# Mamba-2 branch of a hybrid decoder trunk: gates of two groups projected into token rows, with values, outputs and normed outputs turned through VectorE squares and HBM, and dt turned two weights later

## The chip, the cores and the metric

The kernel runs on one core of a Trainium2 chip. The metric is the device time of one execution in microseconds (us), as the median of several runs. A profile is taken of one further execution; its span runs from the first to the last instruction on the core.

Names used below: TensorE (PE in the profile, PEld for its weight loads), VectorE (DVE), ScalarE (ACT), GpSimd (POOL), SyncE (SP).

## The reference

One layer: two parallel token mixers (HGRN2 and Mamba-2), cross-attention into 256 memory tokens, a gated feed-forward block, norms between. All is float32, 256 tokens, model width 2048. The Mamba-2 branch, which is what changes, has 8 groups of 4 heads of 64 values:

```python
xbc = silu(causal_dwconv(xbc_raw, conv_w, conv_b))
xs, bm, cm = split(xbc)                     # 2048 values, 8 x 128, 8 x 128
dt = softplus(dt_raw + dt_bias)             # 32 heads
y = ssd_chunk_scan(xs * dt, dt * A, bm, cm)
y = y + d_skip * xs
y = y * silu(z)
y = y * rsqrt(mean(y * y, over the group's 256 values) + 1e-5)
y = y * norm_g
```

## The kernel before, in words

**Projections.** Each matrix of weights is read once from HBM in pieces of 1 MB (128 rows by 2048 columns), in the order of the list `order` (L87 to L110). `issue` (SyncE) loads a piece two ahead of its use; ScalarE rounds it to a high part (`hi`, L133) and VectorE takes the rest (`lo`, L134), each in two halves of 1024 columns. A pool of five halves holds them, so casts for a piece wait until TensorE has let an earlier half go. TensorE multiplies hi by the hi and lo parts of the activations, and lo by the hi parts.

There are two ways to use a piece. `project` (L241) keeps a 128x128 block of weights in the array and streams tokens: 16 matmuls of 512 columns (the 256 tokens' hi and lo parts side by side) and 16 of 256 columns; the result has channels in rows and tokens in columns, in two halves that `join` (L264) adds: a ScalarE copy `jt` and a VectorE add. `project_tok` (L249) keeps activations in the array and streams 512 columns of weights: over four pieces 96 matmuls of 512 columns, with tokens in rows and no join.

**Order of the work.** Every call of `weights` (one per piece) first runs `step`, which advances the generators in `background` by one stage, and then issues the casts of a later piece. Matmuls that a stage emits are held in their order among themselves; the projections' matmuls, which are not held, are placed around them when the program is built, as are the instructions of the other engines. The result is a fixed order on each engine.

**Mamba-2 before.** `m2_dt` (L661) projects dt for the 32 heads, computes softplus and the running sum, sends the sum to HBM (L680), and has TensorE turn dt and the sum into token rows (L683, L684), with two VectorE copies (L686, L687). `m2_project` (L692) projects six pieces per group: two of values x, one each of B and C, which go through the convolution (L702, L705), and two of gates z. `m2_scan` (L713), a background generator, runs in four stages one or two pieces apart: (A) one Silu over all six (L714) and the decays (L719 to L724); (B) B times C on TensorE (L729, L730), the mask products (L733, L737), a TensorE turn of x into token rows (L742), and x times dt (L745); (C) the 16 matmuls of decays and values (TensorE tile `yp`), d_skip (L759), the product with the gate (L761), squares (L763); (D) a TensorE matmul with ones, which sums the squares over channels (L769), the inverse root (L285, L286), and the norm weights (L773) and the split for the next projection (L281, L282).

**HGRN2**, which the change leaves as it is, already turns its outputs in another way: `turned` (L498) transposes 32x32 squares on VectorE (L503), writes them to HBM by four GpSimd transfers (L506), reads the result back (L509), and `split_turned` (L512) takes it up. Its last head runs beside `m2_dt`.

Of the kernel before, what the change touches and what calls it, by code (L numbers as in the profile page):

```python
# [19 lines left out]
P = 128  # L20
T = 256
# [43 lines left out]
def hybrid_trunk(ctx, tc, xT, memT, par, cst, msk, w_k0, w_ka, w_va, w_hg, w_hv, w_hog, w_ghg, w_bhg, w_dt,  # L65
                 w_m2, w_gm2, w_bm2, w_out, w_q, w_o, w_up, w_dn, fin_g, outT):
# [431 lines left out]
    def turned(y):  # L498

        yq = mp.tile([P, T], F32, name="yq", bufs=1)
        V.transpose(out=yq, in_=y)  # L503
# [4 lines left out]
        yc = mp.tile([P, T], F32, name="yc", bufs=2)  # L508
        G.dma_start(out=yc, in_=yd)  # L509
        return yc  # L510
# [8 lines left out]
    def hg_scan(h, kq, zz, v, sg):  # L519
# [119 lines left out]
        yc = turned(y)  # L639
# [18 lines left out]
    dt_tok = cp.tile([P, 2, 32], F32, name="dt_tok")  # L658
    cum_tok = cp.tile([P, 2, 32], F32, name="cum_tok")

    def m2_dt():  # L661
        ps = project(s2)
        raw = mp.tile([P, T], F32, name="t", bufs=1)
# [5 lines left out]
        V.scalar_tensor_tensor(out=raw[0:32], in0=raw[0:32], scalar=0.0, in1=w[0:32],  # L669
                               op0=ALU.max, op1=ALU.add)  # L670
# [6 lines left out]
        cum = mp.tile([P, T], F32, name="y", bufs=1)  # L677
        V.tensor_tensor_scan(out=cum[0:32], data0=one[0:32], data1=w[0:32], initial=0.0,
                             op0=ALU.mult, op1=ALU.add)
        nc.sync.dma_start(out=cum_d, in_=cum[0:32])  # L680
        ps = pm_.tile([P, 512], F32, name="misc")
        for g in range(2):
            PE.transpose(ps[:, 32 * g:32 * g + 32], raw[0:32, g * P:(g + 1) * P], eye[0:32, 0:32])  # L683
            PE.transpose(ps[:, 64 + 32 * g:96 + 32 * g], cum[0:32, g * P:(g + 1) * P],  # L684
                         eye[0:32, 0:32])
        V.tensor_copy(out=dt_tok, in_=ps[:, 0:64].rearrange("p (g h) -> p g h", g=2))  # L686
        V.tensor_copy(out=cum_tok, in_=ps[:, 64:128].rearrange("p (g h) -> p g h", g=2))  # L687
# [3 lines left out]

    def m2_project(g):  # L692
        sz = mp.tile([P, 6, T], F32, name="sz", bufs=2)
        cb = mp.tile([P, 4, T], F32, name="vc", bufs=2)
        nc.sync.dma_start(out=cb, in_=cum_d[4 * g:4 * g + 4, :].partition_broadcast(P))
        for i in range(4):
            c = m2_chunk(g, i)
            ps = project(s2)
            raw = mp.tile([P, T], F32, name="t", bufs=1)
            join(mp, ps, raw)  # L700
            o = sz[:, i, :]
            S.activation(out=o, in_=raw, func=AF.Identity, bias=pc("m2_cb", c),  # L702
                         scale=pc("m2_cw", 4 * c + 3))
            for s in range(1, 4):
                V.scalar_tensor_tensor(out=o[:, s:T], in0=raw[:, 0:T - s],  # L705
                                       scalar=pc("m2_cw", 4 * c + 3 - s), in1=o[:, s:T],
                                       op0=ALU.mult, op1=ALU.add)
        for i in range(4, 6):
            ps = project(s2)
            join(mp, ps, sz[:, i, :])  # L710
        return sz, cb

    def m2_scan(g, sz, cb):  # L713
        S.activation(out=sz, in_=sz, func=AF.Silu)  # L714
# [10 lines left out]
        yield True  # L725
        yield True
# [12 lines left out]
        tp = pl.tile([P, 512], F32, name="lev")  # L739
        for q in range(2):  # L740
            for i in range(2):
                PE.transpose(tp[:, q * T + i * P:q * T + (i + 1) * P],  # L742
                             sz[:, i, q * P:(q + 1) * P], eye)
        xd = mp.tile([P, 2, T], F32, name="bb", bufs=1)
        V.tensor_tensor(out=xd.rearrange("p q (h c) -> p q h c", c=64),  # L745
                        in0=tp.rearrange("p (q h c) -> p q h c", q=2, c=64),
                        in1=free(dt_tok, 4 * g, [(32, 2), (1, 4), (0, 64)]), op=ALU.mult)
# [9 lines left out]
        y = mp.tile([P, 2, T], F32, name="kq", bufs=2)  # L757
        for i in range(2):
            V.scalar_tensor_tensor(out=y[:, i, :], in0=sz[:, i, :], scalar=pc("m2_d", 2 * g + i),  # L759
                                   in1=yp[:, i * T:(i + 1) * T], op0=ALU.mult, op1=ALU.add)  # L760
        V.tensor_tensor(out=y, in0=y, in1=sz[:, 4:6, :], op=ALU.mult)  # L761
        sq = mp.tile([P, 2, T], F32, name="bb", bufs=1)
        S.activation(out=sq, in_=y, func=AF.Square)  # L763
        V.tensor_tensor(out=sq[:, 0, :], in0=sq[:, 0, :], in1=sq[:, 1, :], op=ALU.add)
        yield True
        if g + 1 < GROUPS:
            yield True
        ps = pm_.tile([P, 512], F32, name="misc")
# [17 lines left out]
    scan = m2_scan(0, *m2_project(0))  # L786
# [14 lines left out]
    for g in range(1, GROUPS):  # L801
        background.append(m2_scan(g, *m2_project(g)))
# [356 lines left out]
def _layout(inp):  # L1159
# [4 lines left out]
    z = _cols(cut(8192, 2048)).reshape(GROUPS, 2, P, 2048)  # L1164
# [20 lines left out]
    def put(name, a):  # L1185
# [35 lines left out]
        "w_m2": np.concatenate([xs, b, c, z], 1), "w_gm2": _toks(cut(16416, 2048)),  # L1221
# [24 lines left out]
```

## Time and profile before

| what | value |
|---|---|
| median of 3 runs | 2253.9 us (2253.28 to 2255.61) |
| the profiled execution: its time, its span | 2255.94 us, 2254.2 us |
| PE busy over the span | 2239.0 us, 99% |
| PEld busy | 1927.9 us, 86% |
| DVE busy | 1623.8 us, 72% |
| ACT busy | 1379.2 us, 61% |
| POOL busy | 45.3 us, 2% |
| mean granted TensorE clock | 0.997 |

Times in the profile are counted from the start of the span. The Mamba-2 branch lies between about 532 us (dt) and 992 us, with the HGRN2 branch's output projections between 578 and 713 us. A row of the timeline gives start, length, engine, line, operation, tile written and tiles read, shapes, and how many were merged; in brackets stands the idle time before it and who ended it. A row of the groups gives line, engine, operation, tiles, shapes, count, busy us, mean ns, and the idle time before with its releasers. The windows give busy us of each engine in a stretch, the granted clock of TensorE, and the DMA share.

### The profile page before, as it was taken

The page shows a single profiled execution, that of the slowest core. Times are in us where ns is not written, and L with a number is a line of the kernel's source. Part 1 is how long each engine was busy: PE and PEld are TensorE (multiplying, and loading weights), DVE is VectorE, ACT ScalarE, POOL GpSimd, SP SyncE. Part 2 cuts the span into 40 slices and gives each one's busy share as a digit, 9 for nine tenths or more (in the row PEclk, how much of TensorE's full clock was granted, in tenths as well). Part 3 has the DMA queues.
Part 4 walks back from the last instruction along what each step waited for, and adds up shares of the span by engine and source line. Part 5 has one row for each costly group of instructions (what it writes and reads, how often), then busy time and mean ns, then how long its engine had stood idle before and what let it go on. Part 6 is the DMA issues. An engine that isn't in the chain of part 4 may idle for free.

```text
span 2254.2 us, 33570 instructions
## 1 busy us (share of the span) xinstructions
PE 2239.0 (99%) x13188; PEld 1927.9 (86%) x13188; DVE 1623.8 (72%) x2602; ACT 1379.2 (61%) x2123; POOL 45.3 (2%) x89
## 2 busy tenths in 40 slices
PE   9999999999999999999999999999999999999998
PEld 8888888887888888888888888888888888888887
DVE  8868878887546677754567765677777777779787
ACT  7567677788546778764456654556555555555554
POOL 0000101100000000000000000000000000000000
PEclk9999999999999999999999999999999999999999
DMA  8645555555655555455566544576555555555554
GB/s 307 245 175 187 183 194 179 182 178 178 219 188 185 189 179 193 180 176 198 187 222 222 210 168 168 178 223 211 193 192 193 193 187 187 188 202 208 207 213 159
DMA packets 89502, 441.11 MB, mean 196 GB/s; under 512 B 25824, under 2 KB 30464, under 8 KB 40320
## 3 DMA queue, kind: packets, MB, share of 16 engines
q1 hardware_dynamic: 69600, 432.36, 53.7%
q0 software_dynamic: 2816, 4.20, 0.7%
q10 hardware_dynamic: 16928, 2.42, 0.6%
q8 instruction: 103, 1.69, 0.3%
q14 instruction: 55, 0.45, 0.1%
HBM read 430.52 MB, written 10.52 MB: 196 GB/s over the span
## 4 chain that ended last, share of the span: by engine, by line
PE 96%; ACT 2%; DVE 1%; issue 0%; DMA 0%; SPq 0%; DVEq 0%
PE proj L82 87%; PE misc L82 5%; PE lev L82 4%; ACT hi L133 0%; DVE lo L134 0%; DMA raw<-in_w_k 0%; DVE e L551 0%; PE lev L811 0%; PE lev L742 0%; ACT L286 0%; ACT L285 0%; ACT h L791 0%; ACT y L638 0%; DVE e L564 0%; PE lev L891 0%
## 5 line engine op out<-in xcount | busy, mean ns | idle before, releaser
L134 DVE TENSOR_TENSOR lo<-raw,hi 128x1024 fp32r<-128x1024 f32 x738 | 894.3, 1223 | 453.2 <-ACT hi L133 403.7
L133 ACT CAST hi<-raw 128x1024 fp32r<-128x1024 f32 x737 | 769.7, 1048 | 425.4 <-PE proj L82 396.6
L82 PE MATMUL proj<-s,hi 128*128 128x512 f32 x3696 | 874.4, 391 | 1.3 <-ACT hi L364 1.1
L82 PEld LDWEIGHTS proj<-s,hi 128*128 128x128 f32 x3696 | 684.9, 188 | 139.2 <-ACT hi L364 2.0
L82 PE MATMUL proj<-hi,s 128*128 128x512 f32 x1962 | 615.2, 390 | 0.0
L82 PEld LDWEIGHTS proj<-s,lo 128*128 128x128 f32 x3696 | 463.6, 191 | 12.1 <-ACT s L281 0.5
L82 PE MATMUL proj<-s,lo 128*128 128x256 f32 x3696 | 471.4, 283 | 0.0
L82 PEld LDWEIGHTS proj<-hi,s 128*128 128x128 f32 x1962 | 368.1, 188 | 76.5 <-issue 0.3
L82 PE MATMUL proj<-lo,s 128*128 128x512 f32 x981 | 382.0, 389 | 0.4 <-DVE lo L134 0.4
L82 PEld LDWEIGHTS proj<-lo,s 128*128 128x128 f32 x981 | 184.2, 188 | 38.2 <-DVE lo L134 0.8
L266 ACT COPY jt<-proj 128x256 f32<-128x256 f32 x183 | 67.7, 370 | 101.4 <-PE proj L82 100.8
L168 ACT CAST hi<-raw 128x1024 fp32r<-128x1024 f32 (+1 forms) x56 | 52.1, 944 | 56.9 <-DVE raw L177 29.9
L169 DVE TENSOR_TENSOR lo<-raw,hi 128x1024 fp32r<-128x1024 f32 (+1 forms) x56 | 60.4, 1088 | 6.6 <-ACT hi L168 5.9
L705 DVE SCALAR_TENSOR_TENSOR sz<-t,par_t,sz 128x255 f32<-128x255 f32 (+2 forms) x96 | 46.2, 481 | 7.4 <-ACT sz L702 5.9
L978 DVE SCALAR_TENSOR_TENSOR gc<-g,par_t,gc 128x255 f32<-128x255 f32 x88 | 42.3, 481 | 2.0 <-ACT gc L976 0.6
L506 POOL DMA_DIRECT2D y_d<-yq x64 | 34.9, 552 | 393.6 <-DVE sm L610 300.2
L82 PE MATMUL proj<-hi,ha 128*128 128x512 f32 x104 | 36.7, 389 | 0.0
L981 ACT ACTIVATE gc<-gc 128x256 f32<-128x256 f32 x44 | 18.4, 417 | 29.9 <-DVE gc L978 29.9
L551 DVE TENSOR_TENSOR e<-bb 128x256 f32<-128x256 f32 x96 | 35.0, 419 | 0.1
L564 DVE TENSOR_TENSOR e<-e,kq 128x256 f32<-128x256 f32 x96 | 34.9, 418 | 0.0
L982 DVE TENSOR_TENSOR gc<-gc,r_f 128x256 f32<-128x256 f32 x44 | 18.7, 425 | 20.9 <-ACT gc L981 20.9
L555 ACT ACTIVATE e<-e 128x768 f32<-128x768 f32 x32 | 27.1, 845 | 10.5 <-DVE e L551 10.0
(302 smaller groups left out, 1765.7 us busy)
## 6 DMA issues: line engine op xcount, KB each, us to landing
raw<-in_w_up SPq DMA_DIRECT2D x88, 1024.0 KB, 4.8
raw<-in_w_m SPq DMA_DIRECT2D x48, 1024.0 KB, 4.8
raw<-in_w_dn SPq DMA_DIRECT2D x44, 1024.0 KB, 4.8
raw<-in_w_hg SPq DMA_DIRECT2D x32, 1024.0 KB, 4.8
raw<-in_w_hv SPq DMA_DIRECT2D x16, 1024.0 KB, 5.0
raw<-in_w_hog SPq DMA_DIRECT2D x16, 1024.0 KB, 4.8
raw<-in_w_ghg SPq DMA_DIRECT2D x16, 1024.0 KB, 4.8
raw<-in_w_bhg SPq DMA_DIRECT2D x16, 1024.0 KB, 4.8
```

The lines of the kernel that those rows point to most:

```text
L82: ins = PE.matmul(*args, **kwargs)
L133: S.copy(out=hi[:, c - a:d - a], in_=raw[:, c:d])
L134: V.tensor_tensor(out=lo[:, c - a:d - a], in0=raw[:, c:d], in1=hi[:, c - a:d - a].bitcast(F32), op=ALU.subtract)
L168: S.copy(out=hi[:, 0:d - c], in_=raw[:, c:d])
L169: V.tensor_tensor(out=lo[:, 0:d - c], in0=raw[:, c:d], in1=hi[:, 0:d - c].bitcast(F32), op=ALU.subtract)
L266: S.copy(out=tmp, in_=ps[:, T:2 * T])
L506: G.dma_start(out=yd.rearrange("(n i) (b f) -> b i n f", i=B, b=P // B)[b], in_=yq[b * B:(b + 1) * B, :].rearrange("i (n f) -> i n f", n=P ...
L551: V.tensor_tensor(out=lev[hw].rearrange("p (n c i) -> p n c i", c=2, i=hw), in0=free(bb, 0, [(2 * hw, nb), (T + hw, 2), (1, hw)]), in1=fre ...
L555: S.activation(out=e[j], in_=e[j], func=AF.Exp)
L564: V.tensor_tensor(out=ev, in0=ev, in1=free(kq, 0, [(2 * hw, nb), (T + hw, 2), (1, hw)]), op=ALU.mult)
L705: V.scalar_tensor_tensor(out=o[:, s:T], in0=raw[:, 0:T - s], scalar=pc("m2_cw", 4 * c + 3 - s), in1=o[:, s:T], op0=ALU.mult, op1=ALU.add)
L978: V.scalar_tensor_tensor(out=gc[:, s:T], in0=g[:, 0:T - s], scalar=pc("f_cw", 3 * c + 2 - s), in1=gc[:, s:T], op0=ALU.mult, op1=ALU.add)
```

## The change

Gates z are no longer projected in `m2_project`. A new `m2_gates` projects the gates of two groups at once with `project_tok` (four pieces), ahead of the even group's values, and the columns are put into an order in which the later squares fit. Silu of the gates is applied in the even group's stage A. Stage A now also turns x: Silu writes x in a mixed order, `turned` transposes its squares, and a GpSimd transfer brings it back in token rows. Stage B takes x times dt from there, with no TensorE turn. Stage C turns the outputs into token rows in the same way, so that the gate, the squares (with a sum along the row) and the inverse root are worked out there with one number for each token, with no matmul with ones. Stage D turns the normed outputs back, and a stage E takes them up with `split_turned`. In `m2_dt`, the turn of dt and its sum into token rows moves to a generator of its own, two pieces later, with its matmuls held in order; `dt_tok` holds each number twice.

```diff
-    order += [w_dt[0]] + [w_m2[0, i] for i in range(6)]
+    order += [w_dt[0]] + [w_z[0, i] for i in range(4)] + [w_m2[0, i] for i in range(4)]
...
-        order += [w_m2[g, i] for i in range(6)]
+        order += [w_z[g // 2, i] for i in range(4) if g % 2 == 0] + [w_m2[g, i] for i in range(4)]
...
-    def turned(y):
+    def turned(y, n, name):
-        yq = mp.tile([P, T], F32, name="yq", bufs=1)
+        yq = mp.tile([P, 64 * n], F32, name="yq", bufs=1)
         V.transpose(out=yq, in_=y)
-        yd = dp.tile([P, T], F32, name="y_d", bufs=4)
+        yd = dp.tile([n * B, T], F32, name=name, bufs=4)
         for b in range(P // B):
             G.dma_start(out=yd.rearrange("(n i) (b f) -> b i n f", i=B, b=P // B)[b],
-                        in_=yq[b * B:(b + 1) * B, :].rearrange("i (n f) -> i n f", n=P // B))
+                        in_=yq[b * B:(b + 1) * B, :].rearrange("i (n f) -> i n f", n=n))
+        return yd
...
         nc.sync.dma_start(out=cum_d, in_=cum[0:32])
+        background.append(m2_dt_rows(raw, cum))
+
+    def m2_dt_rows(raw, cum):
+        yield from pause(2)
         ps = pm_.tile([P, 512], F32, name="misc")
...
+    def m2_gates():
+        zt = mp.tile([P, 2, 512], F32, name="sg", bufs=2)
+        for q, ps in enumerate(project_tok(s2)):
+            S.copy(out=zt[:, q, :], in_=ps)
+        return zt
...
-        for i in range(4, 6):
-            ps = project(s2)
-            join(mp, ps, sz[:, i, :])
...
-    def m2_scan(g, sz, cb):
-        S.activation(out=sz, in_=sz, func=AF.Silu)
+    def m2_scan(g, sz, cb, zt):
+        yield from pause(0 if g in (0, GROUPS - 1) else 1 + 2 * (g % 2))
+        xc = mp.tile([P, 2 * T], F32, name="w", bufs=1)
+        xv = xc.rearrange("p (m i t) -> p i m t", i=2, t=B)
+        S.activation(out=xv, in_=sz[:, 0:2, :].rearrange("p i (m t) -> p i m t", t=B), func=AF.Silu)
+        S.activation(out=sz[:, 2:4, :], in_=sz[:, 2:4, :], func=AF.Silu)
+        if g % 2 == 0:
+            S.activation(out=zt, in_=zt, func=AF.Silu)
+        yd = turned(xc, T // B, "x_d")
+        x = mp.tile([P, 2, T], F32, name="kq", bufs=2)
+        G.dma_start(out=x, in_=yd.rearrange("(q p) c -> p q c", p=P))
...
-        tp = pl.tile([P, 512], F32, name="lev")
...
-                PE.transpose(tp[:, q * T + i * P:q * T + (i + 1) * P],
-                             sz[:, i, q * P:(q + 1) * P], eye)
...
-        V.tensor_tensor(out=y, in0=y, in1=sz[:, 4:6, :], op=ALU.mult)
-        sq = mp.tile([P, 2, T], F32, name="bb", bufs=1)
-        S.activation(out=sq, in_=y, func=AF.Square)
-        V.tensor_tensor(out=sq[:, 0, :], in0=sq[:, 0, :], in1=sq[:, 1, :], op=ALU.add)
...
-        mm(ps[:, 0:T], lhsT=ones, rhs=sq[:, 0, :], start=True, stop=True)
-        r = mp.tile([P, T], F32, name="r", bufs=1)
-        rsqrt(r, ps[:, 0:T], 1.0 / T, eps2_t)
+        yd = turned(y, T // B, "x_d")
+        yt = mp.tile([P, 2, T], F32, name="bb", bufs=1)
+        G.dma_start(out=yt, in_=yd.rearrange("(q p) c -> p q c", p=P))
+        yield from pause(2)
...
+            V.tensor_tensor(
...
+            S.activation(out=yt[:, q, :].rearrange("p (n c) -> p n c", c=B), in_=yv[:, q],
+                         func=AF.Square, accum_out=r[:, q:q + 1])
+        rsqrt(r[:, 2:4], r[:, 0:2], 1.0 / T, eps2_t)
+        for q in range(2):
+            S.activation(out=yv[:, q], in_=yv[:, q], func=AF.Copy, scale=r[:, 2 + q:3 + q])
+        yd = turned(y, T // B, "x_d")
+        yc = mp.tile([P, 2, T], F32, name="yc", bufs=2)
+        G.dma_start(out=yc, in_=yd.rearrange("(i p) t -> p i t", p=P))
+        yield from pause(2)
         for i in range(2):
-            V.scalar_tensor_tensor(out=y[:, i, :], in0=y[:, i, :], scalar=pc("m2_g", 2 * g + i),
-                                   in1=r, op0=ALU.mult, op1=ALU.mult)
-            split(ym[:, 2 * g + i, :], y[:, i, :])
+            split_turned(ym[:, 2 * g + i, :], yc[:, i, :], pc("m2_g", 2 * g + i))
```

**How the order moves.** On TensorE, at dt's projection (`s_76` holds the normed input, `cst_t` the unit matrix, `misc<-vc,a` is an HGRN2 head's last product; the rows with - are of before, with + of after):

```order
 L82 MATMUL proj<-s_76,hi 128x512 x16
-L82 MATMUL proj<-s_76,lo 128x256 x32
-L82 MATMUL proj<-s_76,hi 128x512 x25
-L683 MATMUL misc<-cst_t,t 128x32
-L82 MATMUL proj<-s_76,hi 128x512 x7
-L82 MATMUL proj<-s_76,lo 128x256 x2
-L684 MATMUL misc<-cst_t,y 128x32
-L683 MATMUL misc<-cst_t,t 128x32
-L684 MATMUL misc<-cst_t,y 128x32
+L82 MATMUL proj<-s_76,lo 128x256 x16
 L82 MATMUL misc<-vc,a_1178 128x128 x3
```

The four turns of dt (`t`) and its sum (`y`) leave the middle of the following projection; after, they stand as L687 behind head 15's product, with that head's scores and two pieces of the gates' projection between dt's own matmuls and them.

On VectorE at the same place, before (`t` is dt, `y` the running sum, `lf` a helper):

```order
L665 TENSOR_SCALAR t<-t,par_t 32x256
L134 TENSOR_TENSOR lo<-raw,hi 128x1024
L669 SCALAR_TENSOR_TENSOR t<-t,lf 32x256
L134 TENSOR_TENSOR lo<-raw,hi 128x1024
L673 TENSOR_SCALAR lf<-t,an 32x256
L678 SCALAR_TENSOR_TENSOR y<-r,lf 32x256
L267 TENSOR_TENSOR t<-proj,jt 128x256
L686 COPY dt_tok<-misc 128x64
L687 COPY cum_tok<-misc 128x64
```

and after (`bb` holds dt and its sum, `a` the head's scores):

```order
L618 COPY a_1179<-sm 32x2x32 x4
L669 SCALAR_TENSOR_TENSOR bb<-bb,lf 32x256
L673 TENSOR_SCALAR lf<-bb,an 32x256
L677 SCALAR_TENSOR_TENSOR bb<-r,lf 32x256
L134 TENSOR_TENSOR lo<-raw,hi 128x1024
L502 STREAM_TRANSPOSE yq<-y 128x256
L134 TENSOR_TENSOR lo<-raw,hi 128x1024 x2
L628 TENSOR_TENSOR y<-misc,sg 128x2x4x32
L691 COPY dt_tok<-misc 128x128
L692 COPY cum_tok<-misc 128x64
```

Two `lo` casts stood inside dt's chain, and the next join of a projection behind it had to wait for the turns, which read the same tile `t`. Now no cast stands inside the chain; the first one behind it is the second half of the gates' third piece, and the tile that the turns read is no longer `t`.

On ScalarE in stage A of a group, before (group 4, counting from 0; `e` are the decays, `vc` and `cum_tok` the running sums):

```order
L719 ACTIVATE e_9186<-vc,cum_tok 128x256
L721 ACTIVATE e_9186<-vc,cum_tok 128x128
L719 ACTIVATE e_9186<-vc,cum_tok 128x256
L721 ACTIVATE e_9186<-vc,cum_tok 128x128
L719 ACTIVATE e_9187<-vc,cum_tok 128x256
L133 CAST hi<-raw 128x1024
L721 ACTIVATE e_9187<-vc,cum_tok 128x128
L719 ACTIVATE e_9187<-vc,cum_tok 128x256
L133 CAST hi<-raw 128x1024
L763 ACTIVATE bb<-kq 128x512
L721 ACTIVATE e_9187<-vc,cum_tok 128x128
L724 ACT_TABLE_LOAD
```

and after (group 6: the last twelve rows of the stretch between two casts):

```order
L739 ACTIVATE e_9685<-vc,cum_tok 128x256
L741 ACTIVATE e_9685<-vc,cum_tok 128x128
L739 ACTIVATE e_9685<-vc,cum_tok 128x256
L741 ACTIVATE e_9685<-vc,cum_tok 128x128
L744 ACT_TABLE_LOAD
L744 ACTIVATE e_9684<-e_9684 128x768
L715 ACTIVATE sz<-t,par_t 128x256
L729 ACT_TABLE_LOAD
L729 ACTIVATE sz<-sz 128x512
L744 ACT_TABLE_LOAD
L744 ACTIVATE e_9685<-e_9685 128x768
L133 CAST hi<-raw 128x1024
```

Casts stood among the decays before. In this stretch of after none does: seven rows stand ahead of the twelve shown (four more decays, a table load, a Silu and a convolution start), and four table loads are among the 18 instructions between two casts. Over the whole program the ScalarE order holds 64 table loads, where before's holds 56.

More of the change, by code (lines that the diff above doesn't have):

```diff
@@ L638, in hg_scan @@
             S.activation(out=yv[:, g], in_=yv[:, g], func=AF.Copy, scale=r[:, 2 + g:3 + g])
-        yc = turned(y)
+        yd = turned(y, P // B, "y_d")
+        yc = mp.tile([P, T], F32, name="yc", bufs=2)
+        G.dma_start(out=yc, in_=yd)
         yield from pause(gap)
@@ L662, in m2_dt @@
         ps = project(s2)
-        raw = mp.tile([P, T], F32, name="t", bufs=1)
+        rows = mp.tile([P, 2, T], F32, name="bb", bufs=1)
+        raw, cum = rows[:, 0, :], rows[:, 1, :]
         join(mp, ps, raw)
@@ L680, in m2_dt @@
         nc.sync.dma_start(out=cum_d, in_=cum[0:32])
+        background.append(m2_dt_rows(raw, cum))
+    def m2_dt_rows(raw, cum):
+        yield from pause(2)
         ps = pm_.tile([P, 512], F32, name="misc")
         for g in range(2):
[L683 to L686, printed above, removed]
+            for o, x in ((0, raw), (64, cum)):
+                ins = PE.transpose(ps[:, o + 32 * g:o + 32 * g + 32], x[0:32, g * P:(g + 1) * P],
+                                   eye[0:32, 0:32])
+                tc.keep_in_program_order(ins)
+        V.tensor_copy(out=dt_tok, in_=free(ps, 0, [(32, 2), (1, 32), (0, 2)]))
         V.tensor_copy(out=cum_tok, in_=ps[:, 64:128].rearrange("p (g h) -> p g h", g=2))
@@ L738, in m2_scan @@
                             op=ALU.mult)
-        tp = pl.tile([P, 512], F32, name="lev")
+        xd = mp.tile([P, 2, T], F32, name="bb", bufs=1)
         for q in range(2):
-            for i in range(2):
-                PE.transpose(tp[:, q * T + i * P:q * T + (i + 1) * P],
-                             sz[:, i, q * P:(q + 1) * P], eye)
[L744 to L747, printed above, removed]
+            V.tensor_tensor(out=xd[:, q, :].rearrange("p (i b c) -> p i b c", i=2, c=B),
+                            in0=x[:, q, :].rearrange("p (b i c) -> p i b c", i=2, c=B),
+                            in1=free(dt_tok, 64 * q + 8 * g, [(4, 2), (1, 4), (0, B)]), op=ALU.mult)
         yield True
@@ L762, in m2_scan @@
[L762 to L771 removed]
+            V.scalar_tensor_tensor(out=yv[:, i], in0=xv[:, i], scalar=pc("m2_d", 2 * g + i),
+                                   in1=yp[:, i * T:(i + 1) * T].rearrange("p (m t) -> p m t", t=B),
+                                   op0=ALU.mult, op1=ALU.add)
@@ L772, in m2_scan @@
+        rsqrt(r[:, 2:4], r[:, 0:2], 1.0 / T, eps2_t)
+        for q in range(2):
+            S.activation(out=yv[:, q], in_=yv[:, q], func=AF.Copy, scale=r[:, 2 + q:3 + q])
+        yd = turned(y, T // B, "x_d")
+        yc = mp.tile([P, 2, T], F32, name="yc", bufs=2)
+        G.dma_start(out=yc, in_=yd.rearrange("(i p) t -> p i t", p=P))
+        yield from pause(2)
         for i in range(2):
-            V.scalar_tensor_tensor(out=y[:, i, :], in0=y[:, i, :], scalar=pc("m2_g", 2 * g + i),
-                                   in1=r, op0=ALU.mult, op1=ALU.mult)
@@ L801, in hybrid_trunk @@
     for g in range(1, GROUPS):
[L802 removed]
+        if g % 2 == 0:
+            zt = m2_gates()
+        background.append(m2_scan(g, *m2_project(g), zt))
     def turn(c):
```

31 lines of the change are left out of this document (16 added, 15 removed).

## Prediction

> **What bounds the kernel now.** I read the page's first part, then who waited for whom on TensorE, then the windows of the Mamba-2 stage.
>
> ```profile
> PE 2239.0 (99%) x13188; PEld 1927.9 (86%) x13188; DVE 1623.8 (72%) x2602; ACT 1379.2 (61%) x2123; POOL 45.3 (2%) x89
> ```
> ```profile
> PE misc L683 <- DVE t L669: 3.1, 1, 3.1
> ```
> ```profile
> 756.41:939.57 183.16, 183.16 (x1092) 160.06 (x1091) 137.57 (x211) 145.37 (x215) 0.00 (x0) 1.00 0.51 183
> ```
>
> TensorE is busy 99% of the span, and its longest wait on another engine is one of 3.1 us, at the turn of dt (L683). The window is five Mamba-2 groups of 36.63 us each: TensorE never idles, VectorE is busy 137.57/5 = 27.5 us of a group, ScalarE 145.37/5 = 29.1. So what the change takes off TensorE comes off the span, as long as the two casting engines keep up; ScalarE, with 36.6 - 29.1 = 7.5 us free per group, is the tighter one.
>
> **TensorE, group by group.** A group on TensorE, in starts, lengths and counts:
>
> ```profile
> 757.06 0.60 PE L742 MATMUL lev<-cst_t,sz 128*128 128x128 f32 x4
> 757.42 2.15 PE L82 MATMUL proj<-s,lo 128*128 128x256 f32 x16
> ...
> 772.25 3.82 PE L82 MATMUL proj<-s,hi 128*128 128x512 f32 x16
> 775.91 0.59 PE L82 MATMUL misc<-bb,ones 128*128 128x256 f32 x2
> 776.15 4.03 PE L82 MATMUL proj<-s,hi 128*128 128x512 f32 x16
> 780.01 4.00 PE L82 MATMUL proj<-s,lo 128*128 128x256 f32 x32
> 783.85 7.44 PE L82 MATMUL proj<-s,hi 128*128 128x512 f32 x32
> 791.13 2.08 PE L82 MATMUL proj<-s,lo 128*128 128x256 f32 x16
> ```
>
> Durations of matmuls overlap, so I take distances between starts. 32 lo matmuls take 783.85 - 780.01 = 3.84 us, 32 hi matmuls 791.13 - 783.85 = 7.28 us: a piece in channel rows costs (3.84 + 7.28)/2 = 5.56 us.
>
> A piece in token rows, from a stretch of HGRN2's output projection where each 0.68 us holds three matmuls of 512 columns:
>
> ```profile
> 591.88 0.39 PE L82 MATMUL proj<-lo,s 128*128 128x512 f32 x1
> ...
> 597.32 0.39 PE L82 MATMUL proj<-lo,s 128*128 128x512 f32 x1
> ```
>
> Eight triples lie between the two rows, the 24 matmuls of one piece: 597.32 - 591.88 = 5.44 us.
>
> - Gates: 16 pieces go from channel rows to token rows, 16 x (5.56 - 5.44) = **1.9 us** saved.
> - The four turns of x (L742): 757.42 - 757.06 = 0.36 us per group, eight times: **2.9 us** saved.
> - The matmul with ones: from 772.25 to 780.01 are 7.76 us with 32 hi matmuls, which alone take 7.28; 0.48 us per group, eight times: **3.8 us** saved.
>
> The other matmuls of a group stay. That is 8.6 us; a group costs TensorE 36.63 - 8.6/8 = 35.56 us after.
>
> **dt.** These rows are from the place where dt is turned, and two from a head's block without trouble.
>
> ```profile
> 509.12 0.83 PE L82 MATMUL misc<-vc,a 128*128 128x128 f32 x6
> ...
> 511.36 0.50 PE L82 MATMUL proj<-hi,s 128*128 128x512 f32 x1
> ```
> ```profile
> 532.17 4.00 PE L82 MATMUL proj<-s,lo 128*128 128x256 f32 x32
> 536.01 5.86 PE L82 MATMUL proj<-s,hi 128*128 128x512 f32 x25
> 544.92 0.31 PE L683 MATMUL misc<-cst_t,t 32*128 32x32 f32 x1 [3.06 <-DVE t L669]
> 545.16 3.35 PE L82 MATMUL proj<-s,hi 128*128 128x512 f32 x7
> ...
> 552.43 3.86 PE L82 MATMUL proj<-s,lo 128*128 128x256 f32 x30
> 556.13 2.68 PE L82 MATMUL proj<-s,hi 128*128 128x512 f32 x11
> 559.47 0.91 PE L82 MATMUL misc<-vc,a 128*128 128x128 f32 x6 [0.66 <-DVE a L621]
> ```
> ```profile
> 547.16 0.68 DVE L678 TENSOR_TENSOR_SCAN y<-r,lf 32x256 f32<-32x256 f32 x1
> ```
> ```profile
> 545.00:546.00 1.00, 1.00 (x3) 0.84 (x4) 0.35 (x1) 1.00 (x2) 0.00 (x0) 0.50 0.55 164
> ```
>
> From 532.17 to 552.43 are 20.26 us. In them stand 32 lo (3.84), 32 hi (25 ahead of L683, 7 behind it: 7.28), 2 lo (0.24), the four small turns (at most 0.45), and head 14's product with head 15's scores, which take 511.36 - 509.12 = 2.24 elsewhere: 14.05 us. So 6.2 us are lost: 3.06 of waiting, and the rest because the granted clock (the first 0.50 of the window's row) is half behind the wait: 7 hi take 3.35 us there where full speed makes 1.6. At 559.47 a head's product comes 0.84 us late (11 hi from 556.13 end at 556.13 + 2.50 = 558.63). Together **7.0 us**.
>
> The Trainium skill ("TensorE: Matmul & The Clock Gate", Part 1) has the clock fall to half after an idle window of about 3.4 us; here 3.06 us were enough, and by a strict 3.4 us there would be no slow stretch to win back.
>
> After, the turns stand behind two pieces and the head's block. dt's own matmuls before ended with the first 16 lo, at 532.17 + 1.92 = 534.1; the running sum was there at 547.84, 13.7 us later, with two casts inside its chain that are gone. The turns are due 2.24 + 2 x 5.44 = 13.1 us behind dt's end, and head 15's product (0.83 in the row at 509.12) stands ahead of them too: 13.9 us. So the chain is just covered, at its length of before; I leave 0.5 us for it. The write of the running sum (L680) keeps its place on SyncE's queue at the end of the chain, and the weight loads queued behind it wait no longer than before; its readers (`vc`) stand four pieces later than they did.
>
> Sum of what can go: 1.9 + 2.9 + 3.8 + 7.0 = **15.6 us**.
>
> **What it costs: ScalarE.** Rows of one group (756.41 to 793.04) by mean ns and idle before, then three of HGRN2's last heads:
>
> ```profile
> L266 ACT COPY jt<-proj 128x256 f32<-128x256 f32 x6 | 2.2, 364 | 2.4 <-PE proj L82 2.4
> L714 ACT ACTIVATE sz<-sz 128x1536 f32<-128x1536 f32 x1 | 1.5, 1490 | 0.6 <-DVE sz L267 0.6
> L285 ACT ACT_TABLE_LOAD x1 | 1.3, 1283 | 0.0
> L763 ACT ACTIVATE bb<-kq 128x512 f32<-128x512 f32 x1 | 0.6, 627 | 0.0
> L719 ACT ACTIVATE e<-vc,cum_tok 128x256 f32<-128x256 f32 x4 | 2.0, 496 | 0.0
> L721 ACT ACTIVATE e<-vc,cum_tok 128x128 f32<-128x128 f32 x4 | 1.6, 390 | 0.0
> L724 ACT ACTIVATE e<-e 128x768 f32<-128x768 f32 x2 | 1.7, 848 | 0.0
> L702 ACT ACTIVATE sz<-t,par_t 128x256 f32<-128x256 f32 x4 | 2.4, 600 | 1.8 <-DVE t L267 1.8
> ```
> ```profile
> L515 ACT ACTIVATE jt<-yc,par_t 128x256 f32<-128x256 f32 x2 | 1.0, 510 | 2.9 <-DMA yc<-y_d 2.9
> L635 ACT ACTIVATION_READ_ACCUMULATOR misc<-y 128x1 f32 x4 | 0.7, 186 | 0.0
> L503 DVE STREAM_TRANSPOSE yq<-y 128x256 f32<-128x256 f32 x2 | 0.9, 446 | 2.4 <-ACT y L638 2.4
> ```
>
> Per group it loses two copies (0.73), the Silu of six pieces (1.49) and the Square (0.63): 2.85 us. It gains two Silu of 512 columns (1.26), half a Silu of 1024 (0.63, twice 627 halved), the gates' copy (0.63), two Squares of 256 columns with sums (2 x (0.41 + 0.19) = 1.2; 0.41 is an estimate between the 364 and 510 ns of other 256-column rows), two scalings and two `jt` (4 x 0.51 = 2.04), and one table load (64 against 56 in its order, over eight groups: 1.28): 7.0 us. Net +4.2, so ScalarE needs 33.3 of 35.56 us; 2.3 us are left where 7.5 were. VectorE gains three transposes of 512 columns and loses two joins, the sum of squares and two norm products; even at 0.9 us a transpose (twice the 0.45 of HGRN2's of 256 columns, L503) it needs 27.5 + 2.7 of 35.56 and has room.
>
> The Trainium skill ("ScalarE: Activation LUTs", What ACT_TABLE_LOAD costs) adds about 1380 ns of draining to each 1283 ns load; by that the eight loads cost 1.38 us more per group and 0.9 us are left. The trace shows no such gap: the Exp of L724 follows its load with 0.0 idle.
>
> **What it costs: the way through HBM.** The row of L515 has the one place in before where a result is taken up two pieces after it was sent: ScalarE stood 2.9 us for the transfer, and TensorE did not notice. After, three such ways per group (x, outputs, normed outputs), with twice the bytes, hold VectorE (x times dt; the gate) or ScalarE (`split_turned`). The lower bound is nothing, since the order places casts ahead of them and TensorE has up to 2.5 pieces (13.9 us) cast ahead; the upper is 3 x 2.9 = 8.8 us per group against the 2.3 free. I take one wait in three, 2.9 against 2.3: 0.6 us over, for seven groups in a row 4 us, less where the order fills it; I put 3. GpSimd itself has nothing else queued, and its issues are off the path.
>
> Forecast: 15.6 - 0.5 - 3 = 12 us less: the profiled execution's 2255.94 would be 2243.9. The median of the runs shown is 2253.9, 2.0 lower, so I say **2241.9**.
>
> **Rivals.**
> *(1) dt's stall only moves.* If the chain is 3 us later than 13.9, TensorE waits 3 us and the half clock returns: 6 of the 7.0 us are not won. 2253.9 - 12 + 5.5 = 2247.4. For it: 13.7 against 13.9. Against: the casts inside the chain are gone.
> *(2) ScalarE eats the gain.* Waits of 4.3 us per group, 2.0 over, cost 7 x 2.0 = 14 us: 2253.9 - 15.1 + 14 = 2252.8, no change that counts. For it: 18 instructions stand between two casts in group 6, 12.8 us of work by 8 decays (L719, L721: 3.5), 4 loads (5.1), 2 Silu (1.3), 2 Exp (L724: 1.7) and 2 convolution starts (L702: 1.2), against the 13.9 us of cast pieces.
> *(3) Slower: the three ways bind each group.* All three waits fall on the casting chain: 33.3 + 8.8 = 42.1 us against 35.56, 6.5 us over, seven times 46 us: 2253.9 - 15.1 + 46 = 2285, before any loss of clock. It turns from gain to loss where waits pass 2.3 + 15.1/7 = 4.5 us per group. Against: HGRN2's sixteen ways cost one wait in all, and an engine that is late finds its data landed.
> *(4) All hidden:* 2253.9 - 15.1 = 2238.8, the low side of the forecast.
>
> **How the numbers follow.** Forecast with (4) 0.60, (1) 0.16, (2) 0.12, (3) 0.12. Runs of this kernel differ by 0.1%; 0.2% (4.5 us) is about what can be told from no change, so faster means under 2249.4, slower over 2258.4. Faster: 0.60 + 0.16 = 0.76. Same: 0.12. Slower: 0.12. The low end is (4) less 1.8 for the unknown residue of the half clock elsewhere; the high end takes in (1) and (2): 2237 to 2254, and leaves out (3) and a little on each side.
>
> **What would show it.** Right: no wait at the dt turns (L687 of the new text) and no second of clock 0.50 near 545 us; two groups about 71.1 us apart on TensorE where before had 73.3; ScalarE 93% busy there. Wrong: TensorE rows that wait for `hi` (L133) or `lo` (L134) in the groups, clock windows below 1.00, or ScalarE standing several us for `x_d` transfers in every group.

## The result, and the profile after

The changed kernel takes 2284.9 us (median of 4 runs, 2282.71 to 2286.76) where the kernel before took 2254.8 us beside it: a ratio of 1.0132, with a 95% interval of 1.0120 to 1.0145. It is slower by 30 us; the forecast was 12 us faster.

First part of the page of the changed kernel, busy time of each engine:

```profile
PE 2237.2 (98%) x13012; PEld 1919.1 (84%) x13012; DVE 1625.7 (71%) x2602; ACT 1402.6 (61%) x2191; POOL 118.1 (5%) x209
```

ScalarE is busy 23.4 us longer than before, under the 8 x 4.2 = 33.6 foreseen, and TensorE 1.8 us less, in a span of 2280.9. Most of the loss is TensorE standing. Where, two windows tell, cut at the same matmuls in both kernels: from the last hi matmuls ahead of dt's lo ones to group 1's first channel piece (dt, group 0 and the HGRN2 branch), and from there to the first pieces of the output projection (groups 1 to 7, the Mamba-2 branch). Columns: length, then busy us of PE, PEld, DVE, ACT and POOL, clock, DMA share, GB/s. Before:

```profile
528.55:711.47 182.92, 179.20 (x935) 149.93 (x934) 103.35 (x131) 102.82 (x140) 5.48 (x10) 0.98 0.57 203
711.47:1145.23 433.76, 433.76 (x2322) 371.16 (x2320) 285.86 (x385) 280.36 (x378) 0.00 (x0) 1.00 0.52 185
```

After:

```profile
527.41:722.77 195.36, 190.13 (x963) 158.11 (x962) 108.01 (x135) 107.78 (x146) 10.83 (x19) 0.98 0.58 204
722.77:1172.01 449.24, 421.32 (x2117) 354.13 (x2116) 283.26 (x381) 298.32 (x441) 67.61 (x111) 0.98 0.59 200
```

Group 1's two gate pieces moved from the second window to the first, so the lengths cannot be compared as they stand. By the prediction's terms the first window should have become 182.92 + 4 x 5.44 - 2 x 5.56 - 0.84 - 6.5 = 186.2 us (gates; a turn of x and a matmul with ones; dt), and the second 433.76 - 14 x 5.56 + 12 x 5.44 - 7 x 0.84 = 415.3. They became 195.4 and 449.2: 9.2 and 33.9 us over. TensorE stands 195.36 - 190.13 = 5.2 and 449.24 - 421.32 = 27.9 us of that. The other 3.9 and 6.0 us are matmuls that took longer: the granted clock is 0.98 in both windows, where own_cover (below) shows 1.00 and 186.70 and 415.45 busy us for the same matmuls. What follows the windows is as long as before (2254.2 - 1145.23 = 1109.0; 2280.9 - 1172.01 = 1108.9).

**The groups.** The products of decays and values (`misc<-e,bb`) mark the pace of the groups' own chain. In what follows, a way is one trip through HBM: the square transpose on VectorE, four writes and one read back, up to the use. Timeline of TensorE after, groups 1, 2, 3 and 6, and the two long waits:

```profile
778.65 1.57 PE L82 MATMUL misc<-e,bb 128*64 128x256 f32 x16
823.59 1.86 PE L82 MATMUL misc<-e,bb 128*64 128x256 f32 x16 [0.52 <-DVE bb L760]
870.70 1.72 PE L82 MATMUL misc<-e,bb 128*64 128x256 f32 x16
...
953.98 3.76 PE L82 MATMUL proj<-s,lo 128*128 128x256 f32 x16 [14.26 <-DVE t L267]
...
1006.24 1.85 PE L82 MATMUL misc<-e,bb 128*64 128x256 f32 x16 [0.49 <-DVE bb L760]
...
1077.47 0.77 PE L82 MATMUL proj<-hi,s 128*128 128x512 f32 x1 [5.09 <-ACT s L281]
```

From group 1 to group 6 they are (1006.24 - 778.65)/5 = 45.5 us apart, although TensorE has only 35.6 us of work per group. The projections run ahead of the chain until they cannot, and then wait for most of the lag at once: 14.26 us, after a single wait for `t` of 2.11 us at 863.84. One turn of the chain, from group 2's product to group 3's, in the timeline (DVE, ACT and POOL):

```profile
826.74 0.71 DVE L502 STREAM_TRANSPOSE yq<-kq 128x512 f32<-128x512 f32 x1
827.48 0.61 ACT L728 ACTIVATE w<-sz 128x512 f32<-128x512 f32 x1
...
840.27 0.76 DVE L788 TENSOR_TENSOR kq<-bb,sg 128x256 f32<-128x256 f32 x2 [1.80 <-DMA bb<-x_d]
...
849.06 0.71 DVE L502 STREAM_TRANSPOSE yq<-kq 128x512 f32<-128x512 f32 x1 [1.25 <-ACT kq L796]
850.07 2.32 POOL L505 DMA_DIRECT2D x_d<-yq  x4 [15.96 <-DVE yq L502]
854.62 0.72 POOL L799 DMA_DIRECT2D yc<-x_d  x1 [2.23 <-DMA x_d<-yq]
856.65 0.70 DVE L502 STREAM_TRANSPOSE yq<-w 128x512 f32<-128x512 f32 x1
...
870.09 0.75 DVE L760 TENSOR_TENSOR bb<-kq,dt_tok 128x256 f32<-128x256 f32 x2
```

Group 2's outputs are turned at 826.74 and back from HBM at 840.27, 13.5 us later; gate and norm take until 849.06; the normed outputs are then turned into the same `yq`, which is free when their writes have landed; only then, at 856.65, group 3's x is turned, 28.6 us after its Silu was done (827.48 + 0.61), and it is back at 870.09, 13.4 us later. With 3.2 us from the product to the turn and 0.6 to the next product: 3.2 + 13.5 + 8.8 + 7.6 + 13.4 + 0.6 = 47.1 us. The three ways of a group do not stand beside one another: they queue for one tile. In one turn of the chain are two of them whole and the writes of the third.

How the lag reaches TensorE, on VectorE and ScalarE ahead of 953.98:

```profile
947.74 0.71 DVE L502 STREAM_TRANSPOSE yq<-w 128x512 f32<-128x512 f32 x1 [5.03 <-DMA x_d<-yq]
952.54 0.76 DVE L282 TENSOR_TENSOR s<-jt,s 128x256 fp32r<-128x256 f32 x2 [4.09 <-ACT s L281]
953.41 0.42 DVE L267 TENSOR_TENSOR t<-proj,jt 128x256 f32<-128x256 f32 x1
```
```profile
951.31 0.91 ACT L512 ACTIVATE jt<-yc,par_t 128x256 f32<-128x256 f32 x2 [10.05 <-DMA yc<-x_d]
953.00 0.71 ACT L266 COPY jt<-proj 128x256 f32<-128x256 f32 x2 [0.19 <-DVE s L282]
```

In the fixed order `split_turned` of one group (L512, L282) stands ahead of the joins of the next pieces (L266, L267). ScalarE stands 10.05 us for the normed outputs, VectorE behind it, and no join is done. So the four PSUM tiles `proj` stay full, and TensorE, which is released by the join's add (L267) and not by a cast, has weights but nowhere to put a result.

**dt.** The turn itself (L687, at 547.00) waits for nothing, as foreseen. TensorE's waits come 14 to 31 us later, and ScalarE shows their cause, two heads' ways that it stands for ahead of casts; the granted clock between 555 and 590 is 0.90:

```profile
561.36 1.50 PE L82 MATMUL proj<-s,lo 128*128 128x256 f32 x8 [1.89 <-DVE lo L134]
574.33 1.22 PE L82 MATMUL proj<-s,lo 128*128 128x256 f32 x8 [0.95 <-DVE lo L134]
577.93 1.21 PE L82 MATMUL proj<-s,lo 128*128 128x256 f32 x8 [2.39 <-DVE lo L134]
```
```profile
558.02 0.51 ACT L512 ACTIVATE jt<-yc,par_t 128x256 f32<-128x256 f32 x1 [1.81 <-DMA yc<-y_d]
559.02 1.03 ACT L133 CAST hi<-raw 128x1024 fp32r<-128x1024 f32 x1
...
571.56 0.51 ACT L512 ACTIVATE jt<-yc,par_t 128x256 f32<-128x256 f32 x1 [4.82 <-DMA yc<-y_d]
571.98 1.03 ACT L133 CAST hi<-raw 128x1024 fp32r<-128x1024 f32 x1
```

The same two splits in the kernel before:

```profile
570.94 0.51 ACT L515 ACTIVATE jt<-yc,par_t 128x256 f32<-128x256 f32 x1
580.30 0.51 ACT L515 ACTIVATE jt<-yc,par_t 128x256 f32<-128x256 f32 x1 [2.94 <-DMA yc<-y_d]
```

### The profile page after: what moved, and what is told of

Read it like the earlier page. It is cut to its first block, busy times and chain, and to the rows that moved or that the text cites. A ratio compares the mean times of both kernels' runs of the same rounds, so it can differ in the third digit from the quotient of the medians.

```text
span 2280.9 us, 33510 instructions
## 1 busy us (share of the span) xinstructions
PE 2237.2 (98%) x13012; PEld 1919.1 (84%) x13012; DVE 1625.7 (71%) x2602; ACT 1402.6 (61%) x2191; POOL 118.1 (5%) x209
## 3 DMA queue, kind: packets, MB, share of 16 engines
q1 hardware_dynamic: 69600, 432.36, 53.5%
## 4 chain that ended last, share of the span: by engine, by line
PE 86%; ACT 6%; DVE 3%; DMA 3%; issue 1%; POOL 0%; SPq 0%; DVEq 0%; POOLq 0%; ACTq 0%
PE proj L82 77%; PE misc L82 4%; PE lev L82 4%; DVE lo L134 1%; ACT hi L133 1%; DMA x_d<-yq 1%; DMA yc<-x_d 1%; ACT L286 0%; ACT L285 0%; DMA yc<-y_d 0%; POOL x_d L505 0%; ACT L744 0%; DMA bb<-x_d 0%; DMA kq<-x_d 0%; DVE sz L718 0%
## 5 line engine op out<-in xcount | busy, mean ns | idle before, releaser
L82 PE MATMUL proj<-s,hi 128*128 128x512 f32 x3440 | 813.9, 392 | 0.4 <-DVE lb L432 0.3
L82 PEld LDWEIGHTS proj<-s,hi 128*128 128x128 f32 x3440 | 639.1, 189 | 128.7 <-ACT hi L364 0.9
L82 PE MATMUL proj<-hi,s 128*128 128x512 f32 x2218 | 697.0, 391 | 5.2 <-ACT s L281 5.1
L82 PEld LDWEIGHTS proj<-hi,s 128*128 128x128 f32 x2218 | 416.8, 188 | 93.2 <-ACT s L281 5.5
L82 PEld LDWEIGHTS proj<-s,lo 128*128 128x128 f32 x3440 | 433.7, 192 | 34.6 <-issue 17.1
L82 PE MATMUL proj<-s,lo 128*128 128x256 f32 x3440 | 441.6, 284 | 21.6 <-DVE t L267 16.4
L82 PE MATMUL proj<-lo,s 128*128 128x512 f32 x1109 | 432.7, 390 | 4.4 <-DVE lo L134 4.4
L82 PEld LDWEIGHTS proj<-lo,s 128*128 128x128 f32 x1109 | 208.6, 188 | 47.5 <-DVE lo L134 5.6
L266 ACT COPY jt<-proj 128x256 f32<-128x256 f32 x167 | 61.5, 370 | 86.4 <-PE proj L82 84.0
L505 POOL DMA_DIRECT2D x_d<-yq x96 | 55.7, 587 | 347.5 <-DVE yq L502 329.3
```

Of the source, the lines that this page charges most:

```text
L82: ins = PE.matmul(*args, **kwargs)
L266: S.copy(out=tmp, in_=ps[:, T:2 * T])
```

## The experiments

The theory: x, outputs and normed outputs of all groups share one `yq` (one buffer) and one row of HBM tiles (`x_d`), both handed out in the order of the program, so that group g + 1's x cannot start before group g's normed outputs have gone out; that makes a chain of 45 us per group. The rival: ScalarE's load and three waits per group, as the prediction had it in its rivals (2) and (3).

**own_tiles.** x gets its own tile and its own HBM name. The row of ones is read elsewhere, as the expectation says; own_sbuf has that too.

```diff
-        yq = mp.tile([P, 64 * n], F32, name="yq", bufs=1)
+        yq = mp.tile([P, 64 * n], F32, name=tag, bufs=1)
...
-        yd = turned(xc, T // B, "x_d")
+        yd = turned(xc, T // B, "u_d", "xq")
```

> The changed kernel, with a tile of its own for the turned values x in SBUF and a name of its own for their HBM tile, in place of the yq and x_d that x, outputs and normed outputs share; the row of ones for the running sum of dt is read from the constant ones, which makes the room. Work, transfers and their lengths are as in the changed kernel. Theory (a chain of three ways through one yq and one row of HBM tiles takes 45 us per group, against 35.6 of TensorE): the products with xd come 35 to 36 us apart, the waits at 953.98 (14.26 us) and 1077.47 (5.09 us) go, and some 34 us of the stage from m1 to the branches come back: 2251 us, 2247 to 2258, the loss of the dt stage (8 us) still in it. Rival (ScalarE's work and the length of three ways per group are the limit): both are unchanged, so 2275 us or more.

Measured 2259.3 us (2255.08 to 2264.90), 25.5 us under the changed kernel and 1.3 over the top of the range expected. Between the same matmuls the second window is 422.33 us, 26.9 less than in the changed kernel. The first four products (line numbers are two lower here than in the changed kernel):

```profile
779.80 1.57 PE L82 MATMUL misc<-e,bb 128*64 128x256 f32 x16
815.51 1.57 PE L82 MATMUL misc<-e,bb 128*64 128x256 f32 x16
851.60 1.66 PE L82 MATMUL misc<-e,bb 128*64 128x256 f32 x16 [0.75 <-DVE e L754]
888.90 1.75 PE L82 MATMUL misc<-e,bb 128*64 128x256 f32 x16 [1.45 <-DVE e L754]
```

They are 35.7, 36.1 and 37.3 us apart; the wait of 14.26 us is gone. A wait of 2.9 us at the last group's split stayed, which the theory had said would go. The ways are as many and as long, and ScalarE has the same work: the rival falls.

**own_sbuf.** Only the SBUF tile is x's own; the HBM name stays shared (`turned(xc, T // B, "x_d", "xq")`).

> As own_tiles, but x's way keeps the HBM name x_d that it shares with the outputs: only the SBUF tile is its own. Theory: the transfers of the next group's x still stand behind the normed outputs of the group ahead, the chain shortens from 45 us to no less than 42 per group, still over 35.6: 2265 to 2283 us, with a wait of over 5 us for t or s left on TensorE. If the single SBUF tile alone were the cause: 2251 us. Rival (ScalarE and length of ways): 2275 us or more.

Measured 2282.6 us (2279.26 to 2287.53). The products are 44.8 us apart (from 780.57 to 1004.54 over five groups), and a wait of 9.27 us for t stays. So a tile in SBUF of its own is of little use while its transfer queues under the old name: in the fixed order on GpSimd, x's writes still stand behind the normed outputs'. In own_sbuf:

```profile
829.89 0.71 DVE L502 STREAM_TRANSPOSE xq<-w 128x512 f32<-128x512 f32 x1 [0.72 <-ACT w L726]
850.07 2.32 POOL L505 DMA_DIRECT2D x_d<-yq  x4 [14.14 <-DVE yq L502]
852.38 1.16 POOL L505 DMA_DIRECT2D x_d<-xq  x2
```

and in own_tiles:

```profile
822.80 0.70 DVE L502 STREAM_TRANSPOSE xq<-w 128x512 f32<-128x512 f32 x1
823.79 1.16 POOL L505 DMA_DIRECT2D u_d<-xq  x2 [0.16 <-issue]
```

x's writes go out 21.8 us after its turn in the one, 0.3 us after it in the other. A name of its own in HBM with the shared tile was not run, so whether that alone would do is not shown.

**after_twice** and **cover_twice** lengthen the ways: each read from HBM is issued twice (`G.dma_start(out=x, ...)`, and so for `yt` and `yc`). cover_twice does it to cover_last (below), where each way has its own tile.

> The changed kernel with each of the three reads from x_d of a group issued twice, the second after the first has landed: every way is some 5 us longer, no work on TensorE, VectorE or ScalarE is added. Theory (serial chain through one yq): two of the three reads lie in the chain, 45 us per group becomes some 55, and the last group's chain grows by 15: 60 to 80 us over the changed kernel, 2345 to 2365. Rival (ScalarE's work is the limit): within 10 us of the changed kernel.

> cover_last with the same double reads. Theory: with tiles of their own no chain between two groups is longer than TensorE's 35.6 us even with 5 us more per way (xd to products to outputs to the next x: about 22 + 5), so most of it is hidden: 0 to 15 us over cover_last. Rival (the length of three ways per group counts by itself, whatever the tiles): 60 to 100 us over it.

Measured 2336.5 us (2 runs) and 2267.3 us: 51.6 and 18.7 us more than their kernels. In after_twice the products are (1045.23 - 831.12)/4 = 53.5 us apart, 8 more than in the changed kernel, for two reads in the chain:

```profile
831.12 2.24 PE L82 MATMUL misc<-e,bb 128*64 128x256 f32 x16 [3.86 <-DVE bb L761]
...
1045.23 1.57 PE L82 MATMUL misc<-e,bb 128*64 128x256 f32 x16
```

Both times missed the expectation a little (60 to 80, and 0 to 15): 8 us for two reads make the reads nearer 4 us than 5, and own tiles hide most of the longer ways, not all. Still, the same lengthening costs 2.8 times as much where the ways share a tile, with ScalarE's work unchanged.

**gap4.** HGRN2's last head comes two pieces later (`gap = 4` in place of `4 if h + 1 < HEADS else 2`).

> The changed kernel with the product and the split of HGRN2's last head four pieces after their forerunners, as for the other heads, in place of two. Theory (in the dt stage ScalarE stands 1.8 and 4.8 us for the last two heads' transfers, ahead of casts that TensorE then waits for): waits for lo between 558 and 580 go to under 2 us and the clock there to 1.00: 5 us less, 2280 us (2276 to 2283). Rival (the decays and table loads of group 0 and of dt fill ScalarE there): within 2 us of the changed kernel.

Measured 2281.5 us (2277.27 to 2283.78), 3.4 less; the intervals of the two ratios (1.0115, 1.0100 to 1.0130; 1.0132, 1.0120 to 1.0145) overlap, so the reading rests on the profile. There the first window, between the same matmuls, is 187.96 us, 7.4 less. TensorE's waits between 555 and 590:

```profile
561.43 1.22 PE L82 MATMUL proj<-s,lo 128*128 128x256 f32 x8 [0.56 <-DVE lo L134]
586.62 0.50 PE L82 MATMUL proj<-lo,s 128*128 128x512 f32 x1 [0.69 <-DVE lo L134]
```

They fell from 5.2 to 1.3 us, and the clock is 1.00. The decays and table loads of group 0 are still there, so they were not the cause; the last head's block was. The run moves that head's product, norm and split together and does not part them. The split of the head ahead of it waits even longer than its 1.81 us in the changed kernel, and TensorE only 0.56 us behind it:

```profile
558.67 0.51 ACT L512 ACTIVATE jt<-yc,par_t 128x256 f32<-128x256 f32 x1 [3.71 <-DMA yc<-y_d]
```

**dt_only, dt_gap4, before_gap4.** The dt part alone in the kernel before, the same with `gap = 4`, and `gap = 4` alone there.

> The kernel before with one part of the change: dt and its running sum kept in two rows of bb, and turned two pieces later, with the four turns held in order. Values, outputs and gates as before. By the prediction's term for dt: 7.0 less, 0.5 given back: 2248 us. By what the changed kernel shows (the stall went from the turn to the casts behind the heads' transfers): 2252 to 2258 us, no wait at the turn, and waits for lo some 10 to 30 us behind it.

> dt_only with the last head's product and split four pieces behind: the term for dt by itself, with the transfers of the last heads covered. Theory: TensorE's waits of 2.0, 1.4 and 0.8 us at 562 to 579 in dt_only go and the clock stays at 1.00: 6 to 7 us under the kernel before, 2248 us (2246 to 2250). Rival (the dt chain itself holds the casts): within 2 us of dt_only, 2251 to 2255.

> The kernel before with only the last head's product and split four pieces behind; dt is turned where it was. Theory: the wait of 3.06 us at the turn of dt and the half clock behind it stay, so at most the 0.8 us of a late head's product goes: 2253 to 2255. If the gap alone gave the gain of dt_gap4: 2248.

Measured 2253.1 (ratio 0.9994, 0.9985 to 1.0004), 2253.4 (0.9995, 0.9986 to 1.0004) and 2257.1 us (1.0010, 1.0001 to 1.0019) beside 2254.3 (dt_only) and 2254.6 of the kernel before. So by itself moving the turn of dt cannot be told from no change. In dt_only the waits went to the casts, as said: none at the turn, 2.00 us at 562.94, 1.43 and 0.76 at 577.54 and 578.80. before_gap4 missed its range (2253 to 2255) by 2 us: the wait at the turn stayed (3.07 us), and waits of 1.22 and 0.76 us came at 591.51 and 592.77. dt_gap4 missed the theory's 2248 and fell on its rival's range. Its waits at 562 to 579 did go; instead the last head's split now stands just ahead of the first branch product, with the casts behind it:

```profile
582.40 0.51 ACT L515 ACTIVATE jt<-yc,par_t 128x256 f32<-128x256 f32 x1 [5.94 <-DMA yc<-y_d]
```

TensorE waits 1.70 and 0.76 us behind that, at 587.14 and 588.40, and the clock is 1.00; what else keeps dt_gap4 from 2248 was not traced. In the changed kernel two more gate pieces lie between, the split waits for nothing (589.07 in gap4), and there the gap pays.

**own_gap4.** Both mends together.

> own_tiles and gap4 together: x with its own SBUF and HBM tiles, and the last head's product and split four pieces behind. Theory: two separate losses, so their gains add: 25.5 us (own_tiles) and 5 us (gap4) off the changed kernel's 2284.9, about 2254 us or a little under, 2250 to 2256; left are TensorE's waits of 1.5 + 1.5 + 0.8 us in the groups and 2.9 us at the last group's split. Were both one loss, 2259.

Measured 2250.6 us (2249.09 to 2256.88; ratio 0.9982, 0.9973 to 0.9991). That is 34.3 us under the changed kernel, more than the 25.5 and 3.4 of the medians together, and what the windows gave, 26.9 + 7.4. The waits are those named, but the one at the last split is 7.41 us in the profiled run, the slowest of the eleven.

**four_ways_apart.** On top of it, outputs and normed outputs have a tile and an HBM name each (`x` and `yt` land in the tile they were turned in; `turned(y, T // B, "n_d", "kq")` for the normed outputs).

> own_gap4, and the outputs' and the normed outputs' ways apart as well: x and y land in the tile they were turned in, the turned normed outputs take a slot of kq, and their HBM tile has a name of its own. Theory: in own_tiles the last group's outputs were ready at 989.1 and were turned at 1001.4 only, behind the normed outputs of the group ahead in the one yq; without that the last split comes 8 to 12 us earlier and TensorE's wait of 2.9 us there goes, with the half clock behind it, and some of the 3.7 us in the groups: 3 to 7 us under own_gap4, 2246 to 2251 us. If the ways' length alone held the last group: as own_gap4.

Measured 2251.5 us (2250.08 to 2254.51): no gain over own_gap4. The wait at the split went, as said, but the last group's product now waited 5.49 us for bb. So the last group has a limit of its own: its chain is as long as the work that TensorE has beside it, and mending one place moves the wait to the next.

**cover_last** and **own_cover** put more of that work beside it: three gate projections ahead of the first branch product (`NF = 3`, the third gate in a tile `sg`). cover_last builds on four_ways_apart and has the last product later too; own_cover is own_gap4 with this alone.

> four_ways_apart, with three gate projections instead of two ahead of the first branch product of the Mamba-2 half (NF = 3, the third gate in a tile of sg), and the product with xd of the last group four pieces behind instead of one. Theory: the last group's chain, from the sixth group's products at 953 to the last split at 1024, is as long as what TensorE has to do beside it; 21.8 us more of gates cover it, so the wait of 5.5 us for bb and the half clock behind it go and no wait for s comes: 6 to 9 us under four_ways_apart, 2244 us (2241 to 2247). If the wait only moves to the split: 2249 to 2252.

> own_gap4 with three gate projections ahead of the first branch product (NF = 3), nothing else. Theory: TensorE's wait at the last group's split (2.9 us in own_tiles, 7.4 in the profiled run of own_gap4) goes and the spread of the times with it; the 4.1 us of waits in the groups stay: 2246 us (2244 to 2249).

Measured 2248.6 us (2247.32 to 2251.46) and 2246.2 us (2245.09 to 2246.60). In cover_last the later product put the last split later, and ScalarE stood 9.89 us for it with casts behind: a wait of 2.91 us for hi, a miss. own_cover came as said: 8.4 us under the kernel before, a ratio of 0.9961 (0.9947 to 0.9974). It beats both kernels, and stays 4.3 us over the forecast of 2241.9. Not all that sets it apart from the kernel before is the change: it has `gap = 4` and the third gate too. The kernel before has no standing in its second window that a third gate could fill (433.76 us busy of 433.76), and `gap = 4` alone made it slower. The two windows of own_cover, and groups 1 to 6:

```profile
528.40:716.03 187.63, 186.70 (x963) 155.49 (x962) 107.84 (x135) 108.34 (x147) 10.84 (x19) 1.00 0.60 212
716.03:1135.07 419.04, 415.45 (x2118) 350.94 (x2117) 280.45 (x381) 301.56 (x445) 67.55 (x111) 1.00 0.63 215
```
```profile
771.91:952.11 180.20, 178.14 (x998) 153.19 (x997) 135.80 (x211) 162.69 (x260) 45.56 (x75) 1.00 0.68 227
```

187.63 and 419.04 stand against 186.2 and 415.3 worked out above: 1.4 and 3.7 us over, where the changed kernel is 9.2 and 33.9 over.

## Why the prediction was wrong, step by step

- **TensorE's savings: right.** With the chain out of the way, the second window is 3.7 us over its sum, and TensorE stands 419.04 - 415.45 = 3.6 us of it. A group takes 180.20/5 = 36.0 us with 2.1 us of waits in the five, so 35.6 without; the forecast was 35.56.
- **dt: right at the turn, wrong behind it.** The turn stopped waiting, but rival (1) came true by a way that it did not name: none of the 6.5 us was won, and the first window lost 2.7 more. The last head's split, at a two-piece distance, now reaches ScalarE earlier, before its data (571.56 against 580.30 in the kernel before, with a wait of 4.82 against 2.94 us; dt_only, which takes away the stall at the turn and keeps the rest, has it at 575.59 behind 5.88 us), and the split ahead of it, which had not waited, waits 1.81 us. The prediction had seen the 2.9 us at L515 in the kernel before and noted that TensorE did not notice; it did not ask what stands behind that wait once casts are tight. With `gap = 4` in the changed kernel the first window is within 1.8 us of its sum (187.96 against 186.2).
- **ScalarE: right.** Foreseen were 33.3 us per group; own_cover shows 162.69/5 = 32.5. With the chain apart it does not bind, and rival (2) falls. The Trainium skill ("ScalarE: Activation LUTs", What ACT_TABLE_LOAD costs) would add a drain of about 1380 ns per load. No such gap shows: group 2's gates (L731) have their load at 841.65 for 1.28 us and their Silu at 842.95.
- **The way through HBM: the step that failed.** "The lower bound is nothing ... the upper is 3 x 2.9 = 8.8 us per group against the 2.3 free": each way was priced as a wait on one engine, to be set against that engine's free time, and the sum had 3 us for it. What counts is the length of a chain. A way took 13.4 to 13.5 us from the turn to the use in the turn shown above, and two of them and the writes of the third through one buffer, with gate and norm between, took 45.5 us per group on average against TensorE's 35.6. Taking x out of that chain gave back 25.5 us. The text knew the parts (three ways, `yq` with one buffer in the diff), but never laid the ways of two groups end to end. "GpSimd itself has nothing else queued" was wrong too: in own_sbuf x's writes queue there behind the normed outputs' for 21.8 us.
- **Rival (3) has the number and not the mechanism.** It gave 2285 for three waits on the casting chain in every group. ScalarE waited longer than 3 us for a group's transfer once, for 10.05 us, where the lag came due, and TensorE's longest wait was for the add of a join and not, as the signs of being wrong had it, for `hi` or `lo`; with tiles apart the same three ways cost under 4 us in all. The number agrees by luck.
- **The end of the branch** was not looked at. The last group has no group behind it to hide its chain, and took 5.09 us there (1077.47); a third gate projection ahead hides it.

## What to carry to other kernels

When a change adds round trips, lay one turn of the loop end to end through every buffer that it shares with the next turn, HBM tiles and their names included, and compare the length with the bound engine's time per turn; busy times and single waits don't show it. A chain longer than the turn costs nothing at first, eats the lead of the work ahead of it, and then appears as one long wait in a place that has little to do with it. Where a stall is taken away, ask what it had kept late: that comes early now, and may wait for its data with other work behind it.

## What the runs showed of the hardware

- Transfers of 64 KB from SBUF to HBM (`x_d`) took 3.4 us at the median from issue to landing while 1 MB weight loads ran; all transfers to and from `x_d` took 2.0 to 7.5. With four issues of 0.58 us each on GpSimd, and the read back, the way of 128x512 outputs took 11.8 to 13.5 us in groups 1 to 5 (782.01 to 793.76, 826.74 to 840.27). The Trainium skill ("DMA: Bandwidth & Descriptors", Anatomy of one DMA) gives about 2.0 us and the size over 436 KB per us, an estimate of 2.15 us for such a transfer; the fastest here agrees, the median beside the weight loads does not. The reason is open: the 32 KB writes of `y_d`, beside the same loads, took 1.8 us at the median.
- After the stop of 14.26 us, 16 lo matmuls took 3.55 us (953.98 to 957.53, the next row) where 1.92 is usual: 1.6 us lost to the half clock (0.50 granted in that stretch), a small part of what such a stop costs.
- A short stop can cost nearly as much in clock, and the length of the stop alone does not tell. In the changed kernel the clock was 0.50 behind the stop of 1.89 us at 561.36 (the 32 hi matmuls from 562.66 to 571.30 took 8.64 us where 7.28 is usual), and 1.00 behind those of 2.11 and 2.29 us at 863.84 and 897.07; in gap4 it fell to 0.53 behind one of 2.28 us at 890.75. In the changed kernel:

```profile
563.00:564.00 1.00, 1.00 (x4) 0.72 (x3) 0.94 (x1) 1.00 (x3) 0.00 (x0) 0.50 0.81 328
864.00:866.00 2.00, 2.00 (x17) 2.00 (x17) 1.93 (x4) 0.59 (x2) 0.72 (x1) 1.00 0.71 209
```
